# The first stage of a decoder layer with x in token layout instead of feature layout, and without GpSimd

## The chip, the cores and the metric

The kernel runs on one NeuronCore of a Trainium2 chip, as one launch. The metric is the device time of that launch in microseconds (us). A launch has five engines with queues of their own: TensorE (PE in the profile; its weight loads are PEld), VectorE (DVE), ScalarE (ACT), GpSimd (POOL) and SyncE (SP, which here only issues transfers). Work on different engines is ordered by semaphores alone.

## The reference

One layer (DEPTH is 1) of a decoder trunk on 512 tokens of 1024 features in float32: an adaptive norm, a token mixer (block-sparse attention beside a gated delta rule), a second adaptive norm, a mixture of 32 experts, and a final norm. What matters here is how it begins:

```python
c_act = jax.nn.silu(c)
mod = (c_act @ w_mod[l] + b_mod[l])[:, None, :]
sh1, sc1, g1, sh2, sc2, g2 = jnp.split(mod, N_MOD, axis=-1)
h = rms_norm(x, norm1_w[l]) * (1.0 + sc1) + sh1
# token_mixer(h, ...):
proj = h @ w_in
```

where `rms_norm(x, w)` is `x * rsqrt(mean(x * x) + EPS) * w`, the mean taken over the 1024 features of a token. `w_mod` is 1024 x 6144, and the first 2048 of its columns give `sh1` and `sc1`; `w_in` has 6408 columns.

## The kernel before

The kernel is written in a framework that sets the semaphores itself. It also orders each engine's queue: an instruction may move ahead of others that were written earlier, if its inputs are ready by the framework's own reckoning. `tc.issue_after(i)` holds the instructions of a block behind instruction `i` on the engine of `i`; it sets an order in the queue and is no wait for data.

The program is `mixer` (L805), then the mixture of experts. `mixer` begins with `front` (L223), the stage that is changed. The front makes h for all 512 tokens and multiplies it with the first 768 columns of `w_in`: 512 for the values of the attention, 2 x 128 for the first key and query of the delta rule. What follows is a sequence of units of 128 columns of `w_in` (`unit_in`, L369 and on): 24 matmuls each, into PSUM tiles named `pj`.

Products with `w_in` are made at more than the precision of one pass: each factor is split into a high part of a shorter type (fp32r) and a low part, the rest, and three matmuls are summed: high x high, high x low, low x high (`mm3`, L136). h is kept so as `hhi` and `hlo`, and each piece of the weight as `gh` and `gl`.

The front works in feature layout: the features lie on the partitions, in 8 pieces of 128, and the tokens along the rows.

- x is loaded transposed (`xT`, 128 x 8 x 512) in four transfers of 512 KB, in turn on ScalarE's and SyncE's queue (L248). A row of c, the constants and small columns follow, and then on SyncE's queue, for each piece k, 1 MB of `w_mod` (four buffers, `mr`) and 384 KB of `w_in` (three buffers, `gr`; `w_first` in the profile), L252. After these come the loads of the units (L363).
- c is spread over the partitions by TensorE (L260), and two Silus give `cact` (L273).
- The squares of x's pieces are made on ScalarE (L266) and VectorE (L264), summed in part on VectorE (L268, L270) and over the partitions by TensorE, with a column of ones (L280). `F1` = 12 products before that, `F2` = 5 and `F3` = 8 after it have no result that is used: they keep TensorE's clock up (`warm`, L211).
- The norms come out as 4 columns of 128 tokens, `rs` (L285 to L287). TensorE turns them into rows on all partitions (L292), and ScalarE copies these to `rB` (L293).
- Then a loop over the 8 pieces (L301). For each: ScalarE makes `gh` (L306) and GpSimd `gl` (L307); VectorE makes two products with accumulation over 1024 elements, which are the entries of `mod` for this piece (`mod_tile`, L217 to L220), and two small instructions that give scale and shift (`A1`, L312; `sh1`, L314); GpSimd multiplies the piece of x with `rB` (L317; for piece 0 VectorE does, L321); ScalarE makes h twice, once as `hhi` (L326) and once in full (L327), and VectorE the difference, `hlo` (L328). TensorE does 18 matmuls of 128x128 by 128x512: 12 into `accv` (L332 to L334), 6 into `accf` through `mm3` (L138 to L140).

At the end ScalarE copies `accv` out (L341), and small loads for what follows are issued from ScalarE's queue (L339).

`rsqrt` (L146) is a root on ScalarE and four small instructions on VectorE; `split` (L142) is the pair of ScalarE and VectorE instructions that makes a weight's parts in the later units (L143, L144).

Of the kernel before, what the change touches and what calls it, by code (L numbers as in the profile page):

```python
# [9 lines left out]
F32 = mybir.dt.float32  # L10
# [4 lines left out]
AF = mybir.ActivationFunctionType  # L15
OP = mybir.AluOpType
# [4 lines left out]
D = 1024  # L21
S = 512
EPS = 1e-6
# [12 lines left out]
NU = 18  # L36
SPL = 4
XL = 1
F1, F2, F3 = 12, 5, 8
BA, BB = 0, 1  # L40


# [51 lines left out]
class Prog:  # L94
# [128 lines left out]
    def front(self):  # L223
        tc, nc, I, V = self.tc, self.nc, self.ins, self.view
        v = nc.vector
        mm = nc.tensor.matmul
        pp = self.pf
        hR = self.arena(self.open("H", "right"), "hR", 32, F32R)
        self.hhi, self.hlo = V(hR, 0, [8, 512]), V(hR, 16, [8, 512])
        mp = self.open("MISC", "right")  # L230
        mi = self.arena(mp, "misc", 12)
        self.cm = mp.tile([128, C_W - C_W1], F32, name="cm")
        self.negm = self.cm[:, C_NEG - C_W1:]
        self.va = V(mi, 0, [4, 512])
# [3 lines left out]
        xT = V(sF, 0, [8, 512])  # L238
        rB, nt = V(sF, 16, [512]), V(sF, 18, [512])
        mr = [V(sF, 20 + 8 * i, [2, 1024]) for i in range(4)]  # L240
        gr = [V(sF, 52 + 3 * i, [768]) for i in range(3)]
        sq = [V(sF, 61 + 2 * i, [512]) for i in range(8)]
        one = V(sF, 77, [128])
        crow = V(sF, 78, [1024])[:1]
        v.memset(one, 1.0)
        nc.scalar.activation(nt[:1, 1:2], one[:1, 0:1], AF.Silu)
        nc.sync.dma_start(crow, I["c"])
        for k in range(0, 8, 2):  # L248
            (nc.scalar, nc.sync)[k // 2 % 2].dma_start(xT[:, k:k + 2], I["xT"][:, k:k + 2])
        self.first_loads()  # L250

        def loads(k):  # L252
            if k >= 8:
                return
            nc.sync.dma_start(mr[k % 4], I["w_mod1"][k])
            nc.sync.dma_start(gr[k % 3], I["w_first"][k])
        pc = []
        for b in range(2):
            pc.append(pp.tile([128, 512], F32, name="tr", bufs=2))
            mm(pc[b], one[:1], crow[:, 512 * b:512 * b + 512], start=True, stop=True)  # L260

        for k in range(8):
            if k in (1, 3, 5):
                v.tensor_mul(sq[k], xT[:, k], xT[:, k])  # L264
            else:
                nc.scalar.activation(sq[k], xT[:, k], AF.Square)  # L266
            if k % 2:
                m0 = v.tensor_add(sq[k - 1], sq[k - 1], sq[k])  # L268
            if k in (3, 5):
                m0 = v.tensor_add(sq[0], sq[0], sq[k - 1])  # L270
            if k == 3:
                for b in range(2):
                    nc.scalar.activation(self.cact[:, 512 * b:512 * b + 512], pc[b], AF.Silu)  # L273
        nc.scalar.activation(nt[:1, 0:1], one[:1, 0:1], AF.Sqrt)
        p = pp.tile([128, 512], F32, name="tr", bufs=2)
        w = self.warm(p, one, F1)
        with tc.issue_after(w.ins):
            for t in range(4):
                for k in (0, 6):
                    w = mm(p[:, t:t + 1], sq[k][:, t * 128:(t + 1) * 128], one[:, 0:1], start=k == 0, stop=k == 6)  # L280
        loads(0)
        with tc.issue_after(m0.ins):
            self.mod_tile(0, mr[0][:, 0])
        ss, rs = self.pool.tile([128, 4], F32, name="ss1"), self.pool.tile([128, 4], F32, name="rs1")
        v.tensor_scalar(ss, p[:, 0:4], 1.0 / D, EPS, op0=OP.mult, op1=OP.add)  # L285
        mS = nc.scalar.activation(rs, ss, AF.Sqrt)
        m0 = self.rsqrt(rs, ss, "1", self.pool.tile([128, 4], F32, name="nt1"), root=False)  # L287
        p = pp.tile([128, 4, 128], F32, name="tr", bufs=2)
        with tc.issue_after(w.ins):
            w = self.warm(p[:, 0], one, F2)  # L290
            for t in range(4):
                w = nc.tensor.transpose(p[:, t], rs[:, t:t + 1].to_broadcast([128, 128]), self.ident)  # L292
        mB = nc.scalar.activation(rB, p.rearrange("p a b -> p (a b)"), AF.Copy)  # L293
        accv = [pp.tile([128, 512], F32, name=f"accv{t}") for t in range(4)]
        accf = [pp.tile([128, 512], F32, name=f"accf{t}") for t in range(2)]
        with tc.issue_after(w.ins):
            w = self.warm(accv[0], one, F3)
        ml = None
        with tc.issue_after(m0.ins):
            v.tensor_scalar(self.b1, self.bmod[:, 8:16], 1.0, None, op0=OP.add)  # L300
        for k in range(8):  # L301
# [3 lines left out]
            with tc.issue_after(mB.ins if k else mS.ins):  # L305
                nc.scalar.activation(gh, g, AF.Copy)  # L306
            ml, mg = nc.gpsimd.tensor_tensor(gl, g, gh.bitcast(F32), op=OP.subtract), ml  # L307
            with tc.issue_after(m0.ins):
# [3 lines left out]
            v.tensor_scalar(self.A1[:, k:k + 1], self.mod[:, 8 + k:9 + k], self.b1[:, k:k + 1],  # L312
                            self.n1[:, k:k + 1], op0=OP.add, op1=OP.mult)
            v.tensor_add(self.sh1[:, k:k + 1], self.mod[:, k:k + 1], self.bmod[:, k:k + 1])  # L314
            if k:
                with tc.issue_after(mg.ins):
                    nc.gpsimd.tensor_tensor(xT[:, k], xT[:, k], rB, op=OP.mult)  # L317
            else:
                for a in range(4):
                    c = slice(128 * a, 128 * a + 128)  # L320
                    m0 = v.tensor_mul(xT[:, k, c], xT[:, k, c], p[:, a])  # L321
            h = sq[k]
            ab = dict(scale=self.A1[:, k:k + 1], bias=self.sh1[:, k:k + 1])
            for a in range(1 if k else 4):
                c = slice(0, 512) if k else slice(128 * a, 128 * a + 128)
                nc.scalar.activation(self.hhi[:, k, c], xT[:, k, c], AF.Identity, **ab)  # L326
            m1 = nc.scalar.activation(h, xT[:, k], AF.Identity, **ab)  # L327
            v.tensor_sub(self.hlo[:, k], h, self.hhi[:, k].bitcast(F32))  # L328
            for t in range(4):
                ts = slice(t * 128, t * 128 + 128)  # L330
                with tc.issue_after(w.ins):
                    mm(accv[t], self.hhi[:, k, ts], gh[:, 0:512], start=(k == 0), stop=False)  # L332
                mm(accv[t], self.hhi[:, k, ts], gl[:, 0:512], start=False, stop=False)
                mm(accv[t], self.hlo[:, k, ts], gh[:, 0:512], start=False, stop=(k == 7))  # L334
            for j in range(2):
                cs = slice(512 + 128 * j, 640 + 128 * j)
                self.mm3(accf[j], gh[:, cs], gl[:, cs], self.hhi[:, k], self.hlo[:, k], k == 0, k == 7)
# [1549 lines left out]
```

## Time and profile before

| what | value |
|---|---|
| time, median of 3 runs | 743.18 us (742.13 to 745.19) |
| the profiled execution: its time, its span | 742.16 us, 740.0 us |
| mean granted clock of TensorE, as a share | 0.989 |
| TensorE busy | 707.5 us (96%) |
| VectorE busy | 507.3 us (69%) |
| ScalarE busy | 283.2 us (38%) |
| GpSimd busy | 88.2 us (12%) |
| moved by DMA | 183.11 MB, mean 247 GB/s |
| first and last instruction of the front's loop on TensorE | 18.65 us, 66 us |

A row of the groups gives line, engine, operation, tiles, shape and count, then the busy time in us, the mean of one in ns, and the idle time of the engine just before, with the engine that ended it. A row of the timeline gives start and duration in us, then the same names, and in brackets the idle time before and what ended it. `x4` at the end of a row of the timeline means four instructions merged. A matmul of full f32 shows as two records, one of fp32r as one. In the windows each engine's busy time has the number of its instructions behind it, and the last three columns are granted clock, share of the 16 DMA engines and GB/s. The tile names are those of the memory areas: `sF` holds x, the pieces of `w_mod` and `w_first` and h in full, `sR` the parts of the weight, `hR` those of h, `misc` `cact`.

### The profile page before, as it was taken

Reading aid. Unit: us, or ns where it says so; the run is one execution under the profiler, and the core shown is the slowest. Engines: PE = TensorE matmul, PEld = TensorE weight load, DVE = VectorE, ACT = ScalarE, POOL = GpSimd, SP = SyncE. Lnnn points to the kernel's source line nnn. Section 1 sums busy time; section 2 is a strip of 40 time slices with the busy share of each in tenths; the row PEclk is TensorE's granted clock in tenths of the full one; section 3 lists DMA queues with packets and bytes.
Section 4 is the critical chain, followed back from the end, with each engine's and each line's share of the span. In section 5 each row is a group of like instructions: output and inputs, shape, how many; then the busy total and the mean of one; then the engine's idle time right before and its main releaser. Section 6 shows DMA issues by size and latency. Waiting matters only on the chain. (4 is left out here: it accounts for less than half of the span.)

```text
span 740.0 us, 11015 instructions
## 1 busy us (share of the span) xinstructions
PE 707.5 (96%) x3949; PEld 482.3 (65%) x3949; DVE 507.3 (69%) x1241; ACT 283.2 (38%) x546; POOL 88.2 (12%) x70
## 2 busy tenths in 40 slices
PE   7889999999999989999999999999999999999995
PEld 6657768778877778876768886796444444454431
DVE  5998668987746675668885754256687766677653
ACT  4335445853333312447673233333322222232252
POOL 1863000240222300000000000101010000000000
PEclk9899999999999999999999999999999999999998
DMA  9733222118877661171128897456999999999993
GB/s 357 304 140 116 85 86 86 58 36 286 269 232 279 221 229 58 58 271 42 58 81 292 313 404 315 159 190 240 371 408 409 405 407 411 413 413 406 422 415 153
DMA packets 47515, 183.11 MB, mean 247 GB/s; under 512 B 11802, under 2 KB 13370, under 8 KB 34018
## 3 DMA queue, kind: packets, MB, share of 16 engines
q1 hardware_dynamic: 40690, 169.91, 60.9%
q10 hardware_dynamic: 4896, 8.25, 3.1%
q0 software_dynamic: 1872, 4.23, 1.5%
q8 instruction: 32, 0.52, 0.3%
q14 instruction: 25, 0.20, 0.1%
HBM read 175.63 MB, written 9.33 MB: 250 GB/s over the span
## 5 line engine op out<-in xcount | busy, mean ns | idle before, releaser
L138 PE MATMUL pj<-hR,uR 128*128 128x512 f32 x304 | 122.6, 403 | 1.5 <-DVE qk L736 1.5
L140 PE MATMUL pj<-hR,uS 128*128 128x512 f32 x304 | 122.6, 403 | 0.0
L139 PE MATMUL pj<-hR,uR 128*128 128x512 f32 x304 | 122.4, 403 | 0.0
L143 ACT ACTIVATE uR<-uF 128x1024 fp32r<-128x1024 f32 x48 | 50.8, 1059 | 92.7 <-PE pj L139 81.5
L144 DVE TENSOR_TENSOR uS<-uF,uR 128x1024 fp32r<-128x1024 f32 x48 | 59.7, 1244 | 25.2 <-ACT uR L143 24.8
L1824 DVE TENSOR_TENSOR accF<-accF,cb 128x512 f32<-128x512 f32 x96 | 60.3, 682 | 21.1 <-PE cb L1823 19.9
L1750 PE MATMUL gu<-ra,uS 128*64 128x512 f32 (+1 forms) x344 | 70.2, 597 | 0.0
L138 PEld LDWEIGHTS pj<-hR,uR 128*128 128x128 f32 x304 | 57.3, 189 | 13.6 <-issue 2.7
L140 PEld LDWEIGHTS pj<-hR,uS 128*128 128x128 f32 x304 | 57.3, 189 | 12.6 <-DVE uS L144 1.3
L139 PEld LDWEIGHTS pj<-hR,uR 128*128 128x128 f32 x304 | 57.3, 189 | 11.5 <-issue 0.3
L219 DVE SCALAR_TENSOR_TENSOR sgF<-sgF,misc 128x1024 f32<-128x1024 f32 x32 | 40.1, 1258 | 19.4 <-DMA sgF<-w_mod 19.1
L1750 PEld LDWEIGHTS gu<-ra,uS 128*64 128x64 f32 (+1 forms) x344 | 19.1, 123 | 34.7 <-issue 33.9
L1822 PE MATMUL cb<-uR,oht 128*128 128x512 f32 x96 | 41.1, 428 | 0.0
L1823 PE MATMUL cb<-uR,oht 128*128 128x512 f32 x96 | 37.8, 394 | 0.0
L1807 PE MATMUL cb<-ra,uS 128*32 128x512 f32 (+1 forms) x160 | 36.5, 597 | 0.6 <-ACT uS L1789 0.5
L1812 ACT ACTIVATE uR<-p2F 128x512 fp32r<-128x512 f32 x24 | 15.1, 630 | 56.3 <-DVE p2F L1809 56.3
L1775 ACT ACTIVATE uS<-gu 128x256 f32<-128x256 f32 x13 | 5.0, 384 | 82.3 <-PE gu L1750 82.3
L1636 POOL DMA_INDIRECT uF<-xd,idx x12 | 12.5, 1039 | 180.2 <-PE tr L1671 121.6
L1780 DVE SCALAR_TENSOR_TENSOR uS<-uS,meta,gu 128x256 f32<-128x256 f32 x13 | 6.2, 481 | 34.1 <-ACT uS L1775 34.0
L1750 PE MATMUL gu<-rb,uS 128*32 128x512 f32 (+1 forms) x184 | 29.1, 595 | 0.0
L219 DVE SCALAR_TENSOR_TENSOR sF<-sF,misc 128x1024 f32<-128x1024 f32 x16 | 27.7, 1740 | 0.0
L138 PE MATMUL pj<-mR,uR 128*128 128x512 f32 (+1 forms) x72 | 27.3, 379 | 0.0
(440 smaller groups left out, 1474.8 us busy)
## 6 DMA issues: line engine op xcount, KB each, us to landing
ra<-w_e SPq DMA_DIRECT2D x55, 1024.0 KB, 8.6
rb<-w_e SPq DMA_DIRECT2D x25, 1024.0 KB, 9.4
uF<-w_in SPq DMA_DIRECT2D x38, 512.0 KB, 3.4
sgF<-w_mod SPq DMA_DIRECT2D x32, 512.0 KB, 4.2
rc<-w_e SPq DMA_DIRECT2D x15, 1024.0 KB, 9.1
sF<-w_mod SPq DMA_DIRECT2D x8, 1024.0 KB, 9.0
gd<-sgF ACTq DMA_DIRECT2D x16, 256.0 KB, 2.9
gF<-gd SPq DMA_DIRECT2D x8, 512.0 KB, 3.6
```

The source lines that it names most:

```text
L138: mm(ps, whi, xhi, start=first, stop=False)
L139: mm(ps, whi, xlo, start=False, stop=False)
L140: mm(ps, wlo, xhi, start=False, stop=last)
L143: self.nc.scalar.activation(hi, raw, AF.Copy)
L144: self.nc.vector.tensor_sub(lo, raw, hi.bitcast(F32))
L219: self.nc.vector.scalar_tensor_tensor(raw, raw, 1.0, self.cact, op0=OP.mult, op1=OP.mult, accum_out=self.mod[:, ot:ot + 1])
L1750: nc.tensor.matmul(gu[r], xe[:, k, r], w[:, k % 4], start=k == 0, stop=k == 7)
L1807: nc.tensor.matmul(dn[h][r], aT[:, f, r], w[:, f, c], start=f == 0, stop=f == 1)
L1812: i1 = nc.scalar.activation(self.yhi[:, c], self.yf[:, c], AF.Copy)
L1822: nc.tensor.matmul(pc, self.oht[:, ts], self.yhi[:, c], start=True, stop=False)
L1823: nc.tensor.matmul(pc, self.oht[:, ts], self.ylo[:, c], start=False, stop=True)
L1824: nc.vector.tensor_add(self.acc[:, t, c], self.acc[:, t, c], pc)
```

## The change

x is loaded in token layout (`xr`, 128 tokens x 4 x 1024 features), again in four transfers of 512 KB on the same two queues.

- The sum of squares of a token is then a sum along its row: VectorE makes it for three of the four pieces of 128 tokens, ScalarE for the third, each in one instruction with accumulation. The root's table is loaded behind ScalarE's. The two Silus of c now stand ahead of ScalarE's square.
- The norms stay in token layout: neither ones nor rows of norms are needed. x is scaled by its tokens' norms in two ways. For feature pieces 0 and 1 TensorE multiplies x with a diagonal matrix of the norms (`dg`, four ScalarE instructions), which turns and scales at once, in f32. For pieces 2 to 7 ScalarE scales x in place, in steps 1 to 3 of the loop, two pieces at a time (four instructions 128x256), and TensorE transposes.
- A turned piece lies in PSUM (`tr`, two buffers), and ScalarE makes `hhi` and the full h from there. Piece k + 1 is turned in step k, behind the first six matmuls.
- `gl` is made by VectorE. In its queue it stands behind `A1` and `sh1` of its own step, and the next step's products stand behind it. GpSimd has no work in the front.
- The 18 matmuls of a step are in another order: six high x high, then the four transposes, six high x low, six low x high; all of TensorE's queue in the loop is fixed by hand.
- The warming products are `F1` = 8 ahead of the first turning and `F2` = 10 behind it; the third group is gone. `hf` holds full h in four buffers instead of eight. `xT` is still an input, for use after the mixer.

The diff, cut to its core:

```diff
-F1, F2, F3 = 12, 5, 8
+F1, F2 = 8, 10
...
-        for k in range(0, 8, 2):
-            (nc.scalar, nc.sync)[k // 2 % 2].dma_start(xT[:, k:k + 2], I["xT"][:, k:k + 2])
+        for t in range(4):
+            (nc.scalar, nc.sync)[t % 2].dma_start(xr[:, t], I["xr"][:, t])
...
+        for b in range(2):
+            w = nc.scalar.activation(self.cact[:, 512 * b:512 * b + 512], pc[b], AF.Silu)
+
+        ss, rs = self.pool.tile([128, 4], F32, name="ss1"), self.pool.tile([128, 4], F32, name="rs1")
+        for t in range(4):
+            if t == 2:
+                with tc.issue_after(w.ins):
+                    mS = nc.scalar.activation(jk[0], xr[:, t], AF.Square, accum_out=ss[:, t:t + 1])
             else:
-                nc.scalar.activation(sq[k], xT[:, k], AF.Square)
...
+                v.scalar_tensor_tensor(jk[1], xr[:, t], 1.0, xr[:, t], op0=OP.mult, op1=OP.mult,
+                                       accum_out=ss[:, t:t + 1])
+        with tc.issue_after(mS.ins):
+            nc.scalar.activation(nt[:1, 0:1], one[:1, 0:1], AF.Sqrt)
         loads(0)
...
+        v.tensor_scalar(ss, ss, 1.0 / D, EPS, op0=OP.mult, op1=OP.add)
+        m0 = self.rsqrt(rs, ss, "1", self.pool.tile([128, 4], F32, name="nt1"))
+        for t in range(4):
+            mS = nc.scalar.activation(dg[:, t], self.ident, AF.Copy, scale=rs[:, t:t + 1])
...
+        def turned(k):
+
+            xp[k] = p = pp.tile([128, 512], F32, name="tr", bufs=2)
+            for t in range(4):
+                a, o = xr[:, t, 128 * k:128 * k + 128], p[:, 128 * t:128 * t + 128]
+                if k < 2:
+                    i = mm(o, a, dg[:, t], start=True, stop=True)
+                else:
+                    i = nc.tensor.transpose(o, a, self.ident)
+            return i
+        w = self.warm(accv[0], one, F1)
         with tc.issue_after(w.ins):
-            w = self.warm(accv[0], one, F3)
-        ml = None
+            turned(0)
+            w = turned(1)
+        with tc.issue_after(w.ins):
+            w = self.warm(accv[0], one, F2)
...
-            ml, mg = nc.gpsimd.tensor_tensor(gl, g, gh.bitcast(F32), op=OP.subtract), ml
-            with tc.issue_after(m0.ins):
+            with tc.issue_after(last.ins):
                 for j in range(2):
-                    if k + j:
-                        self.mod_tile(8 * j + k, m[:, j])
...
+                    self.mod_tile(8 * j + k, m[:, j])
...
+            h = hf[k % 4]
+            with tc.issue_after(i.ins), tc.issue_after(j.ins):
+                last = v.tensor_sub(gl, g, gh.bitcast(F32))
+            nc.scalar.activation(self.hhi[:, k], xp[k], AF.Identity, **ab)
+            mS = m1 = nc.scalar.activation(h, xp[k], AF.Identity, **ab)
+            if 0 < k < 4:
+
+                c = slice(256 * k, 256 * k + 256)
+                with tc.issue_after(m1.ins):
+                    for t in range(4):
+                        mS = nc.scalar.activation(xr[:, t, c], xr[:, t, c], AF.Copy, scale=rs[:, t:t + 1])
             v.tensor_sub(self.hlo[:, k], h, self.hhi[:, k].bitcast(F32))
...
+            for a, b, st, sp in ((hi, gh, k == 0, False), (hi, gl, False, False), (lo, gh, False, k == 7)):
+                for t in range(4):
+                    with tc.issue_after(w.ins):
+                        w = mm(accv[t], a[:, k, ts[t]], b[:, 0:512], start=st, stop=sp)
+                for j in range(2):
+                    with tc.issue_after(w.ins):
+                        w = mm(accf[j], b[:, cs[j]], a[:, k], start=st, stop=sp)
+                if b is gh and a is hi and 0 < k < 7:
+                    with tc.issue_after(w.ins):
+                        w = turned(k + 1)
...
+    a["xr"] = f["x"][0].reshape(4, 128, 1024).transpose(1, 0, 2)
```

More of the change, by code (lines that the diff above doesn't have):

```diff
@@ L237, in front @@
         sF, sR = self.arena(st, "sF", 84), self.arena(st, "sR", 18, F32R)
-        xT = V(sF, 0, [8, 512])
-        rB, nt = V(sF, 16, [512]), V(sF, 18, [512])
+        xr = V(sF, 0, [4, 1024])
+        dg, nt = V(sF, 16, [4, 128]), V(sF, 18, [512])
         mr = [V(sF, 20 + 8 * i, [2, 1024]) for i in range(4)]
         gr = [V(sF, 52 + 3 * i, [768]) for i in range(3)]
-        sq = [V(sF, 61 + 2 * i, [512]) for i in range(8)]
+        hf = [V(sF, 61 + 2 * i, [512]) for i in range(4)]
+        jk = [V(sF, 69 + 4 * i, [1024]) for i in range(2)]
         one = V(sF, 77, [128])
@@ L260, in front @@
             mm(pc[b], one[:1], crow[:, 512 * b:512 * b + 512], start=True, stop=True)
-        for k in range(8):
-            if k in (1, 3, 5):
-                v.tensor_mul(sq[k], xT[:, k], xT[:, k])
-            else:
[L266 to L280, printed above, removed]
-        loads(0)
-        with tc.issue_after(m0.ins):
-            self.mod_tile(0, mr[0][:, 0])
-        ss, rs = self.pool.tile([128, 4], F32, name="ss1"), self.pool.tile([128, 4], F32, name="rs1")
@@ L285, in front @@
[L285 to L292, printed above, removed]
@@ L293, in front @@
-        mB = nc.scalar.activation(rB, p.rearrange("p a b -> p (a b)"), AF.Copy)
+        for b in range(2):
[5 more added lines that the diff above has]
+                    mS = nc.scalar.activation(jk[0], xr[:, t], AF.Square, accum_out=ss[:, t:t + 1])
+            else:
+                v.scalar_tensor_tensor(jk[1], xr[:, t], 1.0, xr[:, t], op0=OP.mult, op1=OP.mult,
+                                       accum_out=ss[:, t:t + 1])
@@ L298, in front @@
-        ml = None
+            turned(0)
+            w = turned(1)
+        with tc.issue_after(w.ins):
+            w = self.warm(accv[0], one, F2)
         with tc.issue_after(m0.ins):
             v.tensor_scalar(self.b1, self.bmod[:, 8:16], 1.0, None, op0=OP.add)
+        last = m0
         for k in range(8):
@@ L304, in front @@
             gh, gl = V(sR, 6 * (k % 3), [768]), V(sR, 3 + 6 * (k % 3), [768])
-            with tc.issue_after(mB.ins if k else mS.ins):
+            with tc.issue_after(mS.ins):
                 nc.scalar.activation(gh, g, AF.Copy)
-            ml, mg = nc.gpsimd.tensor_tensor(gl, g, gh.bitcast(F32), op=OP.subtract), ml
-            with tc.issue_after(m0.ins):
+            with tc.issue_after(last.ins):
                 for j in range(2):
-                    if k + j:
-                        self.mod_tile(8 * j + k, m[:, j])
@@ L312, in front @@
[L312 to L321, printed above, removed]
@@ L322, in front @@
-            h = sq[k]
-            ab = dict(scale=self.A1[:, k:k + 1], bias=self.sh1[:, k:k + 1])
[L324 to L334, printed above, removed]
@@ L335, in front @@
-            for j in range(2):
-                cs = slice(512 + 128 * j, 640 + 128 * j)
-                self.mm3(accf[j], gh[:, cs], gl[:, cs], self.hhi[:, k], self.hlo[:, k], k == 0, k == 7)
+                    self.mod_tile(8 * j + k, m[:, j])
+            j = v.tensor_scalar(self.A1[:, k:k + 1], self.mod[:, 8 + k:9 + k], self.b1[:, k:k + 1],
+                                self.n1[:, k:k + 1], op0=OP.add, op1=OP.mult)
+            i = v.tensor_add(self.sh1[:, k:k + 1], self.mod[:, k:k + 1], self.bmod[:, k:k + 1])
@@ new lines, in front @@
+            v.tensor_sub(self.hlo[:, k], h, self.hhi[:, k].bitcast(F32))
+            ts = [slice(t * 128, t * 128 + 128) for t in range(4)]
+            cs = [slice(512 + 128 * j, 640 + 128 * j) for j in range(2)]
+            hi, lo = self.hhi, self.hlo
+            for a, b, st, sp in ((hi, gh, k == 0, False), (hi, gl, False, False), (lo, gh, False, k == 7)):
[8 more added lines that the diff above has]
+                        w = turned(k + 1)
```

1 line of the change is left out of this document (added).

## The prediction

> **What bounds the kernel now.** I read the page first, then its windows cut at the borders of the front, then the groups of instructions inside the front with their shapes kept apart, and last the timeline.
>
> ```profile
> span 740.0 us, 11015 instructions
> ```
>
> The profiled execution took 742.16 us, 2.2 us around a span of 740.0; the median of the three runs is 743.18, so 1.0 us is added at the end to a sum made on this execution.
>
> ```profile
> 18.65:65.99 47.34, 39.46 (x145) 29.70 (x145) 43.76 (x67) 20.65 (x31) 29.85 (x15) 0.89 0.53 197
> 65.99:480.00 414.01, 405.18 (x2072) 317.23 (x2071) 285.20 (x669) 180.27 (x338) 42.29 (x38) 1.00 0.51 177
> ...
> 520.00:720.00 200.00, 199.46 (x1284) 89.68 (x1281) 135.20 (x320) 56.35 (x125) 10.26 (x10) 1.00 1.00 409
> ```
>
> The columns are the stretch, its length, busy time of PE, PEld, DVE, ACT and POOL, the granted clock, the DMA share and GB/s. From 18.65 (first matmul of the front's loop) to 65.99 (first matmul behind it) VectorE is busy 43.8 of 47.3 us, while TensorE idles 7.9 us and has a clock of 0.89. Everywhere else TensorE fills the time: 405 of 414 us, then 199 of 200. So the front is the one long stretch that TensorE does not pace, and the question is what paces it.
>
> ```profile
> L219 DVE SCALAR_TENSOR_TENSOR sF<-sF,misc 128x1024 f32<-128x1024 f32 x16 | 27.7, 1740 | 0.0
> L307 POOL TENSOR_TENSOR sR<-sF,sR 128x768 fp32r<-128x768 f32 x8 | 19.1, 2392 | 26.7 <-DVE rs L156 15.8 <-issue 8.3 <-ACT sR L306 2.5
> L314 DVE TENSOR_TENSOR sh<-mod,c_cols 128x1 f32<-128x1 f32 x8 | 9.0, 1120 | 0.0
> ...
> L306 ACT ACTIVATE sR<-sF 128x768 fp32r<-128x768 f32 x8 | 6.6, 830 | 0.0
> L327 ACT ACTIVATE sF<-sF,sh,A 128x512 f32<-128x512 f32 x8 | 6.4, 801 | 0.0
> ```
>
> ```profile
> 25.70 1.21 DVE L219 SCALAR_TENSOR_TENSOR sF<-sF,misc 128x1024 f32<-128x1024 f32 x1
> 26.85 1.22 DVE L219 SCALAR_TENSOR_TENSOR sF<-sF,misc 128x1024 f32<-128x1024 f32 x1
> 28.00 0.68 DVE L328 TENSOR_TENSOR hR<-sF,hR 128x512 fp32r<-128x512 f32 x1
> 28.22 2.14 POOL L307 TENSOR_TENSOR sR<-sF,sR 128x768 fp32r<-128x768 f32 x1 [2.45 <-ACT sR L306]
> 28.60 0.26 DVE L312 TENSOR_SCALAR A<-mod,b,c_cols 128x1 f32<-128x1 f32 x1
> 28.78 1.59 DVE L314 TENSOR_TENSOR sh<-mod,c_cols 128x1 f32<-128x1 f32 x1
> ...
> 33.14 2.86 DVE L219 SCALAR_TENSOR_TENSOR sF<-sF,misc 128x1024 f32<-128x1024 f32 x1
> ...
> 60.41 0.15 DVE L314 TENSOR_TENSOR sh<-mod,c_cols 128x1 f32<-128x1 f32 x1
> 60.52 0.27 DVE L312 TENSOR_SCALAR A<-mod,b,c_cols 128x1 f32<-128x1 f32 x1
> 60.71 1.21 DVE L144 TENSOR_TENSOR uS<-uF,uR 128x1024 fp32r<-128x1024 f32 x1
> ```
>
> The two products at 25.70 and 26.85, with GpSimd idle, take 1.15 us from start to start; the one at 33.14, beside GpSimd's subtraction, takes 2.86. A 128x1 addition takes 0.15 at 60.41 and 1.59 at 28.78, where GpSimd had started 0.56 before. VectorE's instructions are stretched whenever GpSimd runs: 16 x (1.74 - 1.22) = 8.3 us on the products and 8 x (1.12 - 0.15) = 7.8 on the small additions, 16 of its 44 busy us. The additions give the shift that ScalarE needs for h, so each stretched one delays h and with it TensorE.
>
> ```profile
> 24.69 2.08 PE L334 MATMUL accv<-sR,hR 128*128 128x512 f32 x4 [3.21 <-DVE hR L328]
> ...
> 33.20 0.39 PE L140 MATMUL accf<-hR,sR 128*128 128x512 f32 x1
> ...
> 35.92 0.39 PE L334 MATMUL accv<-sR,hR 128*128 128x512 f32 x1
> ...
> 50.54 0.50 PE L332 MATMUL accv<-sR,hR 128*128 128x512 f32 x1 [2.00 <-ACT hR L326]
> ...
> 51.26 0.63 PE L332 MATMUL accv<-sR,hR 128*128 128x512 f32 x1
> ...
> 51.69 0.63 PE L333 MATMUL accv<-sR,hR 128*128 128x512 f32 x1
> ```
>
> ```profile
> 25.00:30.00 5.00, 5.00 (x13) 3.89 (x13) 5.00 (x8) 2.25 (x3) 2.55 (x2) 0.50 0.79 297
> ...
> 50.00:55.00 5.00, 4.46 (x13) 3.50 (x14) 4.49 (x8) 1.93 (x3) 2.94 (x2) 0.66 0.00 0
> ```
>
> At full clock 12 matmuls start between 33.20 and 35.92: 0.227 us each. The loop's 144 then cost 32.6 us. The other 14.7 of 47.3 are 7.9 of idling and 6.8 that come with it: after the waits of 3.21 and 2.00 us the clock falls to half, and a matmul takes 0.43 (51.26 to 51.69).
>
> **The change, part by part.**
>
> *GpSimd leaves.* Its 8 subtractions go to VectorE, its 7 products with the norm disappear: x is now scaled by its own row, and ScalarE and TensorE do that. VectorE's step, unstretched, is two products 2.30, A1 and shift 0.30, h's low part 0.60 (28.00 to 28.60) and a new subtraction of 128x768. That shape is not in the trace on VectorE; it lies between 0.68 (512 wide) and 1.21 (1024 wide), midway 0.95. Sum 4.15 a step, 33.2 for eight.
>
> *ScalarE's step.* The split of the weight 0.83, two makings of h at 0.80 each. h now comes from PSUM; the nearest rows give 0.80 (the same form from SBUF) and 0.60 below (a plain 128x512 copy from PSUM), so 2.0 to 2.4. In steps 1 to 3 four scalings 128x256 come on top:
>
> ```profile
> L768 ACT ACTIVATE aF<-aF,sm 128x256 f32<-128x256 f32 x8 | 4.0, 504 | 0.4 <-DVE sm L767 0.4
> ```
>
> 2.0 us at most, hence 4.4 in three of the steps. What is queued behind them is the next weight split; VectorE's subtraction waits for that, but I expect slack there (below).
>
> *TensorE's step.* The 18 matmuls stay, in another order: 4.08 us. Steps 1 to 6 add four transposes each, turning the next piece.
>
> ```profile
> 156.12 1.14 ACT L617 ACTIVATE dF<-ax,nk 128x128 f32<-128x128 f32 x4 [3.42 <-PE ax L615]
> ...
> 156.62 1.47 PE L615 MATMUL ax<-ct,dF 128*128 128x128 f32 x12
> ```
>
> Twelve such take 1.47, so four 0.49. A full step is 4.57 us, above VectorE's 4.15 and ScalarE's 4.4: **TensorE becomes the pace of the loop**. Eight steps: 32.6 + 6 x 0.49 = 35.6 us. Waits that the new order brings are covered: the transposes of step 1 follow six matmuls (1.4 us) and wait for ScalarE's scalings, 0.8 + 2.0 us behind h's high part of that step; that high part is ready long before TensorE gets there, because TensorE starts late (next paragraph). If the cover were gone it would cost 1.4 us, once. GpSimd's subtraction as a wait of the weight queue goes too:
>
> ```profile
> SPq L256 <- POOL sR L307: 26.3, 5, 7.0
> ...
> SPq L975 <- PE gu L1750: 63.8, 22, 7.0
> ```
>
> The loads of w_first stood 26.3 us in SP's queue behind it, and the w_in loads behind them; both come earlier. The count and sizes of x's loads, and their two queues, are as before.
>
> *The start.*
>
> ```profile
> 2.29 3.75 PE L260 MATMUL tr<-sF 1*128 1x512 f32 x4 [2.29 <-DMA sF<-c]
> ...
> 7.01 1.06 ACT L273 ACTIVATE misc<-tr 128x512 f32<-128x512 f32 x2
> ...
> 7.64 5.49 PE L214 MATMUL tr<-sF 128*128 128x128 f32 x24 [1.61 <-ACT misc L273]
> 7.96 1.67 ACT L266 ACTIVATE sF<-sF 128x512 f32<-128x512 f32 x3
> ...
> 9.65 1.28 ACT L274 ACT_TABLE_LOAD   x1
> ...
> 15.02 0.16 DVE L285 TENSOR_SCALAR ss<-tr 128x4 f32<-128x4 f32 x1 [2.39 <-PE tr L280]
> ...
> 16.06 0.16 DVE L156 SCALAR_TENSOR_TENSOR rs<-nt,rs 128x4 f32<-128x4 f32 x1
> ...
> 16.77 1.95 PE L214 MATMUL accv<-sF 128*128 128x128 f32 x16
> ```
>
> The row sums need no TensorE any more. All of x is in by about 8.5 (the second of the three squares from 7.96 reads the last piece). VectorE's last square ends near 9.7. ScalarE's stands behind the two Silus, which end at 8.07: about 1.2 us for 1024 elements, then the table load of 1.28, at 10.6. From the scaled sum to the norm the chain takes 16.22 - 15.02 = 1.2, of which 0.2 lies before the root: norm at 11.8 instead of 16.2. Four diagonals follow at 1.14/4 each, the first ready at 12.1. Then TensorE has 18 f32 products of 128x128 in a fixed order ahead of the loop (turning pieces 0 and 1, and ten that only warm the clock). One costs 1.95/8 = 0.244 at full clock and 5.49/12 = 0.457 in the cold start. Bounds: all warm 4.4 us, loop from 16.5 (h is ready by 11.8 + 2 x 1.15 + 0.5 + 0.8 = 15.4). But TensorE has idled over 2 us by then, and the windows show half clock for 3.4 us (a clock of 0.66 over 5 us) to over 5 us after such waits: 3.4 us of cold, then full, gives 6.0; 5.3 gives 6.9; loop from 18.1 to 19.0. Worse still: the eight warming products F1 depend only on a memset and may run ahead of the products with c, which start at 2.29; that can delay those, the Silus and the norm by up to 8 x 0.457 - 1.3 = 2.4, loop from 21.4. I take 19.0, beside the 18.65 of before: what the early norm gains, the warming eats.
> The Trainium skill ("TensorE: Matmul & The Clock Gate", Part 1) says that the clock is halved after at least one idle window of about 3.4 us and released after about 3.4 us of sustained work. The trace halves it after only 2.00 us of idling, and shows the 3.4 us once and a longer stretch once; by the page's release time the loop would start at 18.1 and the result be 0.9 us lower.
>
> *Sum.* 19.0 + 35.6 = 54.6 against 65.99: 11.4 us. Behind it, VectorE's and ScalarE's splits of the first w_in units fall due at the same distance before the end of the loop, and they have slack. The stages after are TensorE's own (405 of 414 us). Between 520 and 720 the DMA share is 1.00 at 409 GB/s, but those loads are issued when TensorE's work frees their buffers (the SP row with gu above), so they move with it. 742.16 - 11.4 = 730.8, and 1.0 for the median: **731.8 us**.
>
> **Rivals.**
> 1. *VectorE's queue stays serial.* If the next step's products are queued behind h's low part and the subtraction, a step is h 0.8, low part 0.6, subtraction 0.95, products 2.3, A1 and shift 0.3, h's high part 0.8: 5.75. TensorE would then end near 15.4 + 7 x 5.75 + 4.1 = 59.8: 6.2 us gained, 737.0. Against it: in the trace the next products run ahead of h's low part. Chance 0.10.
> 2. *The gain is lost later*, because a later stretch is tied to transfers (DMA 1.00 over 200 us): half, 737.5. For it speaks that share, against it the issue waits. Chance 0.07.
> 3. *The change does not do what it says*: VectorE's stretching comes from the DMA's writes, not from GpSimd. Then VectorE keeps its 5.5 us a step (43.8/8) and gets 0.95 more: 11.8 + 8 x 6.45 + 2 = 65.4, no change, 743. Against it: the rows at 25.70 and 26.85 are short, with the DMA share of 0.79 in that window. Chance 0.05.
> 4. *Slower: the half clock.* If the weight split also gets into the serial chain (it is queued behind h and behind the scalings), a step is 5.75 + 0.83 = 6.6, TensorE idles 2.0 us in every step, and 2.00 was enough for the clock to fall. It then stays low: 18 x 0.43 + 0.5 = 8.2 us a step, 19.0 + 66 = 85, 19 us slower, 762. It decides from 6.6 us a step on. Chance 0.06. By the same section of the Trainium skill it would take 3.4 us of idling, so a step of 8 us, and this rival would be all but excluded; the measured 2.00 keeps it in.
>
> **How the numbers follow.** The forecast has 0.72: its own range runs from a loop start at 16.5 (729.3) to one at 21.4 (734.2), widened by the runs' spread to 728.3 to 735.5. The first two rivals, 737.0 and 737.5, are faster as well. The range must leave out no more than two in ten; up to 738.0 it holds all but rivals 3 and 4 and some of the tails. 0.5%, which is about what a measurement of this kernel can tell from no change, is 3.7 us. Faster 0.88, same 0.06, slower 0.06.
>
> **What would show it.** Right: no GpSimd work between 1 and 54 us; the products with w_mod at 1.2 us, the shift additions at 0.15; TensorE busy without a gap from about 19 to 55 at a clock of 1.00; the first matmul on w_in near 55 instead of 66, and the same 674 us behind it. Wrong: products still at 1.7; waits of TensorE for h over 1 us in each step; half clock inside the loop; a transpose that waits for ScalarE's scalings; or a tail that grew.

## The result and the profile after

The changed kernel took 731.6 us (median of 4 runs, 728.54 to 733.87) beside 742.98 us for the kernel before (4 runs): 11.4 us less, a ratio of 0.984 with a 95% interval of 0.982 to 0.987. Two later comparisons of the same two kernels gave 0.983 [0.980, 0.986] and 0.981 [0.977, 0.985].

The first two lines of the page after are the span and the busy time of each engine:

```profile
span 732.1 us, 11015 instructions
...
PE 702.7 (96%) x3955; PEld 483.2 (66%) x3955; DVE 495.8 (68%) x1242; ACT 286.0 (39%) x555; POOL 54.9 (7%) x55
```

The profiled execution took 733.87 us; it was the slowest of the four, at a mean granted clock of 0.988 where the other three had 0.994 to 0.997, and why it was is a question of its own below. GpSimd has 33 us less to do than before. VectorE has 11.5 us less although it took over GpSimd's eight subtractions. Now the windows, cut as in the prediction: the loop of the front, the units behind it, a stretch of the experts (length, PE, PEld, DVE, ACT, POOL, clock, DMA share, GB/s):

```profile
17.08:52.76 35.68, 35.68 (x172) 29.48 (x170) 31.55 (x71) 22.16 (x36) 0.00 (x0) 1.00 0.76 296
52.76:467.00 414.24, 403.58 (x2055) 317.26 (x2054) 285.98 (x668) 179.82 (x339) 41.20 (x38) 0.99 0.51 176
507.00:707.00 200.00, 197.25 (x1266) 89.73 (x1266) 135.76 (x319) 54.99 (x125) 10.25 (x10) 1.00 0.99 403
```

In the loop TensorE is busy for all of the 35.68 us, at a clock of 1.00. Before it was busy for 39.5 of 47.3 us at 0.89. So TensorE paces the loop now, and VectorE has 4 us to spare. In the two other stretches TensorE is still busy nearly all the time; that it is a little less so than before (403.6 of 414 us at a clock of 0.99, and 197.3 of 200) belongs to the question of what this execution lost behind the front. The groups of the first 53 us, shapes kept apart, show what became of VectorE's instructions:

```profile
L219 DVE SCALAR_TENSOR_TENSOR sF<-sF,misc 128x1024 f32<-128x1024 f32 x16 | 19.2, 1219 | 0.0
...
L318 DVE TENSOR_TENSOR sR<-sF,sR 128x768 fp32r<-128x768 f32 x8 | 7.6, 953 | 0.4 <-ACT sR L308 0.4
...
L319 ACT ACTIVATE hR<-tr,sh,A 128x512 fp32r<-128x512 f32 x8 | 6.2, 780 | 10.9 <-PE tr L292 7.8 <-DVE A L312 3.1
...
L314 DVE TENSOR_TENSOR sh<-mod,c_cols 128x1 f32<-128x1 f32 x8 | 1.2, 152 | 0.0
```

The sixteen products fell from 1740 to 1219 ns, the eight shift additions from 1120 to 152 ns, and the subtraction of 128x768 that came to VectorE takes 953 ns. The same in VectorE's timeline, one step of the loop:

```profile
15.18 1.22 DVE L219 SCALAR_TENSOR_TENSOR sF<-sF,misc 128x1024 f32<-128x1024 f32 x1
...
16.32 0.69 DVE L327 TENSOR_TENSOR hR<-sF,hR 128x512 fp32r<-128x512 f32 x1
16.93 1.22 DVE L219 SCALAR_TENSOR_TENSOR sF<-sF,misc 128x1024 f32<-128x1024 f32 x1
...
18.07 0.15 DVE L314 TENSOR_TENSOR sh<-mod,c_cols 128x1 f32<-128x1 f32 x1
...
18.38 0.95 DVE L318 TENSOR_TENSOR sR<-sF,sR 128x768 fp32r<-128x768 f32 x1
19.25 1.22 DVE L219 SCALAR_TENSOR_TENSOR sF<-sF,misc 128x1024 f32<-128x1024 f32 x1
```

A step is 4.07 us (15.18 to 19.25), and the first product of the next step is issued ahead of the low part of h: the queue is not serial. Last, TensorE's timeline:

```profile
1.06 3.36 PE L214 MATMUL accv<-sF 128*128 128x128 f32 x14 [1.06 <-DVE sF L246]
4.35 1.98 PE L261 MATMUL tr<-sF 1*128 1x512 f32 x4
...
11.71 3.38 PE L290 MATMUL tr<-sF 128*128 128x128 f32 x16 [4.96 <-ACT sF L279]
14.93 2.40 PE L214 MATMUL accv<-sF 128*128 128x128 f32 x20
17.08 1.17 PE L334 MATMUL accv<-sR,hR 128*128 128x512 f32 x4
...
22.63 0.60 PE L292 MATMUL tr<-ct,sF 128*128 128x128 f32 x4
...
52.76 0.39 PE L138 MATMUL pj<-hR,uR 128*128 128x512 f32 x1
```

The last row is the first matmul on `w_in` behind the front: 52.76 instead of 65.99, a gain of 13.2 us at that point. Only 7.9 us of it are left in the span of this execution (740.0 to 732.1). So 5.3 us were given back on the way, and that had to be explained.

### The profile page after: what moved, and what is told of

The parts are those of the page before. It is cut to its first block, busy times and chain, and to the rows that moved or that the text cites. A ratio compares the mean times of both kernels' runs of the same rounds, so it can differ in the third digit from the quotient of the medians.

```text
span 732.1 us, 11015 instructions
## 1 busy us (share of the span) xinstructions
PE 702.7 (96%) x3955; PEld 483.2 (66%) x3955; DVE 495.8 (68%) x1242; ACT 286.0 (39%) x555; POOL 54.9 (7%) x55
## 5 line engine op out<-in xcount | busy, mean ns | idle before, releaser
L139 PEld LDWEIGHTS pj<-hR,uR 128*128 128x128 f32 x304 | 57.6, 189 | 11.6 <-issue 0.3
L219 DVE SCALAR_TENSOR_TENSOR sgF<-sgF,misc 128x1024 f32<-128x1024 f32 x32 | 41.9, 1316 | 18.3 <-DMA sgF<-w_mod 18.2
L1815 ACT ACTIVATE uR<-p2F 128x512 fp32r<-128x512 f32 x24 | 15.1, 630 | 56.2 <-DVE p2F L1812 56.2
L409 DVE SCALAR_TENSOR_TENSOR dF<-dF,c_cols 128x512 f32<-128x512 f32 x36 | 26.5, 748 | 0.9
L140 PE MATMUL pj<-mR,uS 128*128 128x512 f32 (+1 forms) x72 | 27.0, 375 | 0.0
```

The lines of the kernel that those rows point to most:

```text
L139: mm(ps, whi, xlo, start=False, stop=False)
L140: mm(ps, wlo, xhi, start=False, stop=last)
L219: self.nc.vector.scalar_tensor_tensor(raw, raw, 1.0, self.cact, op0=OP.mult, op1=OP.mult, accum_out=self.mod[:, ot:ot + 1])
L409: nc.vector.scalar_tensor_tensor(a, r[:, k:k + 512], w[:, k:k + 1], a, op0=OP.mult, op1=OP.add)
```

## The experiments

Three questions were open: what stretched VectorE, how much each half of the change brings, and where the 5.3 us went. A fourth came with the start of the loop. The ratio is to the runs of the kernel before in the same comparison; the three last columns, in us, come from one profiled execution each; "tail" is the span less the front's end, that is, all that lies behind the first matmul on `w_in`.

| kernel | median, us (runs) | ratio to before | loop starts | front ends | tail |
|---|---|---|---|---|---|
| before | 742.98 (4) | 1 | 18.65 | 65.99 | 674.0 |
| after | 731.60 (4) | 0.984 [0.982, 0.987] | 17.08 | 52.76 | 679.3 |
| after_again | 730.89 (6) | 0.983 [0.980, 0.986] | 18.44 | 54.11 | 674.4 |
| pool_beside | 748.28 (5) | 1.007 [1.004, 1.009] | 22.24 | 72.50 | 673.4 |
| feature_dve | 732.98 (4) | 0.987 [0.983, 0.990] | 18.71 | 57.62 | 673.5 |
| short_warm | 728.82 (4) | 0.980 [0.977, 0.983] | 15.90 | 52.56 | 676.7 |
| sub_on_pool | 733.92 (4) | 0.988 [0.986, 0.990] | 17.18 | 56.10 | 674.3 |
| pool_one_input | 745.63 (10) | 1.004 [1.002, 1.005] | 20.95 | 68.66 | 674.6 |
| warm_bridge | 729.60 (5) | 0.983 [0.981, 0.986] | 15.59 | 51.78 | 674.3 |
| no_warm | 729.35 (4) | 0.982 [0.980, 0.984] | 15.47 | 51.51 | 673.3 |
| after_third | 730.29 (6) | 0.981 [0.977, 0.985] | 18.07 | 53.74 | 675.0 |
| no_warm_again | 728.28 (6) | 0.980 [0.976, 0.984] | 15.85 | 51.80 | 673.4 |

**The changed kernel once more** (after_again, no edit): does the give-back belong to the change or to that one execution?

> The changed kernel once more, with five rounds and a second profile. In the first profile the front ended 13.2 us earlier than before, but the span was only 7.9 us shorter: 5.3 us were given back, 4.5 of them in the stage that inverts the triangular blocks, where TensorE waited 2.40 and 2.06 us and the clock fell to half twice. Theory: that is a matter of each execution's transfers and clock windows, not of the change; this profile gives back under 3 us there, the time is 728 to 733, and the front ends at 52.8 again within 0.3. Rival: the earlier front makes the inversion collide with the loads of w_mod in every execution; then this profile gives back 4 to 5 us there again, at the same two waits.

The tail was 674.4 us, 0.4 more than before's; it was 675.0 in a third profile. So the give-back does not come with every execution of the change, and the medians keep the whole gain: they lie 13.2 and 13.6 us below the kernel before in the two later comparisons, where the fronts end 11.9 and 12.3 us earlier. What the first profile had lost can be read: two waits of TensorE for VectorE in the inversion of the triangular blocks of the delta rule. Behind both stands a load: shortly before, a product with `w_mod` in VectorE's queue had waited 1.20 and 3.02 us for its transfer. First after's rows, those of VectorE ahead of those of TensorE, and then the windows of 6 us around the waits:

```profile
236.93 1.23 DVE L219 SCALAR_TENSOR_TENSOR sgF<-sgF,misc 128x1024 f32<-128x1024 f32 x1 [1.20 <-DMA sgF<-w_mod]
...
254.35 1.23 DVE L219 SCALAR_TENSOR_TENSOR sgF<-sgF,misc 128x1024 f32<-128x1024 f32 x1 [3.02 <-DMA sgF<-w_mod]
```

```profile
238.81 0.66 PE L608 MATMUL ax<-ct,dF 128*128 128x128 f32 x4 [2.40 <-DVE dF L605]
...
256.50 0.49 PE L650 MATMUL ax<-dF 128*128 128x128 f32 x2 [2.06 <-DVE dF L647]
```

```profile
238.00:244.00 6.00, 5.18 (x28) 4.80 (x29) 3.41 (x8) 1.20 (x2) 1.38 (x1) 0.72 0.64 214
256.00:262.00 6.00, 5.50 (x26) 4.89 (x27) 3.71 (x9) 0.00 (x0) 0.00 (x0) 0.72 0.56 182
```

The clock was 0.72 in both windows, which costs up to 0.28 x 6 = 1.7 us in each. The repeat has the first of these waits too, almost as long, and its clock stays full:

```profile
239.96 0.66 PE L608 MATMUL ax<-ct,dF 128*128 128x128 f32 x4 [2.27 <-DVE dF L605]
```

```profile
239.00:245.00 6.00, 5.04 (x36) 4.43 (x37) 4.35 (x8) 1.79 (x3) 2.68 (x2) 1.00 0.63 215
```

Two falls of the clock are 3.4 us; one wait for a weight of the experts near 697 us, 1.4 us in the first profile and 0.2 in the repeat, is 1.2; that makes 4.6 us, and TensorE's waits in the inversion are 7.2 us in sum in the first profile and 6.2 in the repeat, one more. The tails differ by 4.9, so the parts are right to about a microsecond. That the earlier front has no part in such waits is not shown: waits of over 2 us stand in this stage in four profiles with the changed front (after, after_again, short_warm, sub_on_pool) and not in the one profile of before, whose longest is 1.03. Whether a wait of 2 us costs the clock is no matter of its length alone. The Trainium skill ("TensorE: Matmul & The Clock Gate", Part 1) says that the window in which activity is counted runs freely and so meets the same kernel in another phase each time. That fits 2.27 us at a clock of 1.00 beside 2.40 us at 0.72; its figure of 3.4 us of idling does not fit this trace, which has idle times of 2.40 and 2.06 there.

The expected front's end was missed, by 1.3 us. The rows of TensorE in the repeat show why:

```profile
4.34 3.78 PE L261 MATMUL tr<-sF 1*128 1x512 f32 x4
...
12.69 3.76 PE L290 MATMUL tr<-sF 128*128 128x128 f32 x16 [3.84 <-ACT sF L279]
...
18.44 1.17 PE L334 MATMUL accv<-sR,hR 128*128 128x512 f32 x4
```

The products with c took 3.78 us instead of 1.98: here they ran at half clock, and Silu, norm and turning came 1 us later. The start of the loop is not fixed to better than about 1.4 us.

**GpSimd's work put back, on other data** (pool_beside): is it GpSimd that stretches VectorE's instructions, or the DMA's writes (rival 3)? Nothing of the computation changes; nobody reads the results of the added instructions.

```diff
+        for n in range(16):
+            c = slice(0, (768, 512)[n % 2])
+            nc.gpsimd.tensor_tensor(jk[1][:, c], jk[1][:, c], jk[0][:, c], op=OP.subtract)
         last = m0
```

> The changed kernel, and beside its loop 16 GpSimd subtractions of the two sizes that GpSimd had before (8 of 128x768, 8 of 128x512), on data that nothing else uses, so that no instruction waits for GpSimd. Theory (GpSimd's running alone stretches VectorE, and that paced the front): the products with w_mod go from 1.22 to about 1.7 us each while GpSimd works, VectorE's loop gets 10 to 18 us longer, TensorE waits again, the front ends at 58 to 66 instead of 52.8 and the time is 736 to 744. Rival (what cost was waiting for GpSimd's results, or the late norm, or the order of the matmuls; the stretching is the DMA's): the front ends at 53 to 54 and the time stays within 2 us of the changed kernel's.

The front ended at 72.50, and the kernel is slower than before. Its groups in the front and its window of the loop:

```profile
L219 DVE SCALAR_TENSOR_TENSOR sF<-sF,misc 128x1024 f32<-128x1024 f32 x16 | 25.7, 1624 | 0.0
...
L304 POOL TENSOR_TENSOR sF<-sF 128x768 f32<-128x768 f32 x8 | 18.1, 2257 | 10.1 <-DVE sF L271 9.6
...
L317 DVE TENSOR_TENSOR sh<-mod,c_cols 128x1 f32<-128x1 f32 x8 | 5.5, 682 | 0.0
```

```profile
22.24:72.50 50.26, 40.83 (x171) 32.13 (x170) 46.52 (x75) 22.52 (x37) 20.13 (x10) 0.90 0.50 181
```

One of the small instructions that make the norm, ahead of the loop:

```profile
10.04 1.80 DVE L276 TENSOR_SCALAR ss<-ss 128x4 f32<-128x4 f32 x1
```

Nobody waits for the added work, and yet the products are back at 1.62 us and the additions at 0.68. The loop takes 50.3 us instead of 35.7, with 9.4 us of waits of TensorE for h and a clock of 0.90, much as before the change. All of these waits lie before 43.1, where the added work ends; behind that TensorE is busy without a gap. The DMA share in the loop is lower than after's (0.50 against 0.76). So the stretching is GpSimd's, and rival 3 falls. The size was underestimated, though VectorE's busy time in the loop grew by 15.0 us, within the 10 to 18 expected. The front ends 19.7 us later than after's, and the expectation left out two parts of that: the loop starts 5.2 us later (22.24 against 17.08), since the added work meets the norm's small instructions as well (1.80 us at 10.04 where the changed kernel has 0.16; the norm is ready at 15.1 against 11.2), and a clock of 0.90 over 50.3 us is about 5.0 us. The waits are the other 9.4.

**The old layout without GpSimd** (feature_dve): the kernel before, in which VectorE makes the subtraction and the product of x with the norms.

```diff
-            ml, mg = nc.gpsimd.tensor_tensor(gl, g, gh.bitcast(F32), op=OP.subtract), ml
+                    v.tensor_mul(xT[:, k], xT[:, k], rB)
...
-                    nc.gpsimd.tensor_tensor(xT[:, k], xT[:, k], rB, op=OP.mult)
+                last = v.tensor_sub(gl, g, gh.bitcast(F32))
```

> The kernel before in its feature layout, with one part of the change alone: GpSimd's subtractions and its products with the norms go to VectorE. Theory: VectorE's step is then 4.15 + 0.61 = 4.76 us, without stretching, from the norm at 16.2 on: eight steps, h 0.8 and the last 18 matmuls 4.1 end the front at 58 to 59, so 7 to 8 us of the 13.2 come from freeing VectorE alone and the time is about 735. The layout gives the rest: the earlier norm, and the product with the norm off VectorE. Rival (the token layout, with its early norm and the new matmul order, is what gains): the front ends at 63 to 67 and the time is 740 to 744.

The window of its loop, and two rows of VectorE's timeline one step apart:

```profile
18.71:57.62 38.91, 36.27 (x145) 26.09 (x145) 37.18 (x75) 21.39 (x31) 0.00 (x0) 1.00 0.66 240
```

```profile
27.98 0.95 DVE L322 TENSOR_TENSOR sR<-sF,sR 128x768 fp32r<-128x768 f32 x1
...
32.64 0.95 DVE L322 TENSOR_TENSOR sR<-sF,sR 128x768 fp32r<-128x768 f32 x1
```

VectorE is busy 37.2 of 38.9 us: it still paces the loop, at 4.66 us a step, but unstretched and with no half clock. The front ended 8.4 us earlier than before (57.62), a little better than expected. In time the kernel is at 732.98, 2.1 us behind the changed one of the same comparison, with intervals that overlap. So in the old layout, too, taking GpSimd's work away brings most of the gain.

**The new layout with GpSimd's subtraction** (sub_on_pool): the other half alone.

```diff
-            with tc.issue_after(i.ins), tc.issue_after(j.ins):
-                last = v.tensor_sub(gl, g, gh.bitcast(F32))
+            last = i
+            nc.gpsimd.tensor_tensor(gl, g, gh.bitcast(F32), op=OP.subtract)
```

> The changed kernel with one part undone: the 8 subtractions that make the low part of the weight are on GpSimd again, 2.0 to 2.4 us each; the products with the norm stay away from it. Theory (a VectorE instruction beside a GpSimd one takes up to as long as the GpSimd one): VectorE loses 8 x 0.87 = 7.0 us of its own work and gains about 0.5 us of stretching for each of 16 to 19 us of GpSimd, 8 to 9.5; its loop stays near TensorE's 35.7, so the front ends at 53 to 58 and the time is 730 to 736. Rival (any two-input work of GpSimd brings the old pace back): the front ends above 60, the time is above 738.

The front ended at 56.10, within what was expected. One collision in the timelines of VectorE and GpSimd:

```profile
28.31 1.21 DVE L219 SCALAR_TENSOR_TENSOR sF<-sF,misc 128x1024 f32<-128x1024 f32 x1
...
29.45 1.79 DVE L314 TENSOR_TENSOR sh<-mod,c_cols 128x1 f32<-128x1 f32 x1
```

```profile
28.95 2.28 POOL L318 TENSOR_TENSOR sR<-sF,sR 128x768 fp32r<-128x768 f32 x1 [1.11 <-ACT sR L308]
```

The product was running when GpSimd began at 28.95, and kept its 1.21 us. The 128x1 addition behind it started in the middle of GpSimd's instruction and ended at 31.24; GpSimd ended at 31.23. It waited that instruction out. In the groups the additions are stretched as before the change (mean 1128 ns), the products much less (1316 instead of 1740). Either half alone ends the front 8 to 10 us earlier, both together 12 to 13: the halves overlap. Either takes GpSimd's product with the norms away, and with both TensorE's 35.7 us set the loop, so that what VectorE has to spare counts for nothing.

**GpSimd work with one input** (pool_one_input): is it two inputs on GpSimd's side that matter?

```diff
+        for n in range(24):
+            nc.gpsimd.tensor_copy(jk[1], jk[0])
         last = m0
```

> The changed kernel, and beside its loop 24 GpSimd copies of 128x1024 on data that nothing else uses. Each reads one tensor instead of two. Theory (what GpSimd and VectorE get in each other's way with is the reading of two tensors): the products with w_mod stay at 1.22 us, the front ends at 52.5 to 54.5, the time stays within 2 us of the changed kernel's. Rival (any GpSimd work on SBUF stretches VectorE): the products take 1.5 us and more, the front ends above 58 and the time is above 735, as with the 16 subtractions, which gave 72.5 and 748.

The groups in the front:

```profile
L303 POOL COPY sF<-sF 128x1024 f32<-128x1024 f32 x24 | 36.8, 1535 | 11.2 <-DVE sF L271 9.7
...
L219 DVE SCALAR_TENSOR_TENSOR sF<-sF,misc 128x1024 f32<-128x1024 f32 x16 | 26.7, 1686 | 0.0
...
L316 DVE TENSOR_TENSOR sh<-mod,c_cols 128x1 f32<-128x1 f32 x8 | 4.5, 562 | 0.0
...
L314 DVE TENSOR_SCALAR A<-mod,b,c_cols 128x1 f32<-128x1 f32 x8 | 2.1, 264 | 0.0
```

My theory fell: plain copies on GpSimd stretch VectorE's products to 1.69 us and cost the whole gain (745.63). So two inputs on GpSimd's side are not needed, and what remains is VectorE's side. Its two-tensor instructions wait, while `A1`, which reads one tensor and two scalars by pointer, stays at 0.26 us beside any GpSimd work in these fronts. The number of tensors is not the whole rule, though. The one-tensor instruction at 10.04 in pool_beside took 1.80 us instead of 0.16, and behind the front, in the changed kernel itself, a one-tensor instruction of 128x512 (L407, at 55.26) that meets a GpSimd memset takes 2.03 us, where the median of its line is 0.48. What tells such instructions from `A1` was not tested. The Trainium skill ("GPSIMD Engine Reference", section 8) says that the two engines share their interfaces to SBUF, the memory of the tiles, and that VectorE's instructions contend which have two SBUF inputs or run in a 2-port perf mode. The two-tensor rows agree with it; the mode of an instruction no trace here shows. The size of the effect is what these runs add.

**The warming products.** Three kernels change only their numbers. short_warm cuts the group between turning and loop:

```diff
-F1, F2 = 8, 10
+F1, F2 = 8, 1
```

> The changed kernel with one warming product instead of ten behind the first turning (F2 = 1). In the first profile h's first piece was ready at 15.3, but TensorE did the warming until 17.0. Theory: the loop starts at 15.3, the clock is already full by then (it rose at 14.5), the front ends 1.7 us earlier, at 51.1, and the time is 1 to 2 us lower. Rival: the ten products are what brings the clock up; without them the loop's first 3.4 us or more run at half clock, and the front ends at 52.8 or later.

The loop's first rows:

```profile
12.04 3.78 PE L290 MATMUL tr<-sF 128*128 128x128 f32 x16 [5.29 <-ACT sF L279]
...
15.90 2.05 PE L334 MATMUL accv<-sR,hR 128*128 128x512 f32 x4
```

The loop started at 15.90, but its first four matmuls took 2.05 us instead of 1.17: the clock was still at half. So the end was 52.56 and not the 51.1 expected. The long tail of this profile, 676.7, is like that of the first: TensorE waited 2.88 us for VectorE ahead of 240.11, and the clock was 0.58 over 240 to 244. warm_bridge makes the wait for x itself warm instead:

```diff
-F1, F2 = 8, 10
+F1, F2 = 24, 5
```

> The changed kernel with 24 and 5 warming products instead of 8 and 10: 17 of the 24 fill TensorE's time between c's products and the first turning. With one product behind the turning the loop had started at 15.9 but ran its first 2 us at half clock. Theory: the clock is full from about 8 us on, the turning takes 2.0 instead of 3.4 us, the loop starts when h is there, at 15.3 to 16.5, at full clock, the front ends at 51.0 to 52.2 and the time is 727.5 to 729.5. Rival: the 17 products run at half clock, 7.8 us, and hold the turning up; the loop starts at 18 or later and nothing is gained against the changed kernel.

```profile
6.15 5.69 PE L214 MATMUL accv<-sF 128*128 128x128 f32 x34
12.01 2.05 PE L290 MATMUL tr<-sF 128*128 128x128 f32 x16 [0.17 <-ACT sF L279]
...
15.59 1.21 PE L334 MATMUL accv<-sR,hR 128*128 128x512 f32 x4 [0.41 <-ACT hR L319]
```

That held: the turning takes 2.05 us at full clock instead of 3.4 to 3.8, and TensorE then waits 0.41 us for h, so this is the earliest start that h allows here; the front ended at 51.78. The time, 729.60, is just above the 727.5 to 729.5 expected. no_warm has almost no warming at all:

```diff
-F1, F2 = 8, 10
+F1, F2 = 1, 1
```

> The changed kernel with one warming product in each place instead of 8 and 10. Theory (warming only decides where the half clock falls): c's products run at half clock, 3.7 us, from 2.3; the turning runs at half clock, the loop starts at 15.5 to 16.5 and its first 3 to 6 us run at half clock, which costs 1.5 to 3 us; the front ends at 52.5 to 55 and the time is 729 to 733. Rival (the warming is what the front needs): the clock stays low for long, TensorE falls behind, the front ends above 57.

```profile
2.27 3.78 PE L261 MATMUL tr<-sF 1*128 1x512 f32 x4 [0.42 <-DMA sF<-c]
11.61 3.78 PE L290 MATMUL tr<-sF 128*128 128x128 f32 x16 [5.56 <-ACT sF L279]
15.19 0.64 PE L214 MATMUL accv<-sF 128*128 128x128 f32 x2
15.47 1.51 PE L334 MATMUL accv<-sR,hR 128*128 128x512 f32 x4
```

It was better than expected: 51.51. The products with c start at 2.27 instead of 4.35, since nothing stands ahead of them; they and the turning run mostly at half clock, but that holds nothing up: ScalarE makes h's high part from 14.45 on, and what it waits for last is VectorE's `A1`, not the turned piece. At 15.47 h is there and the loop starts at once. The cold costs 0.34 us on the first four matmuls. The changed kernel and this one were then compared once more, side by side:

> The changed kernel beside the one without warming products, on the same chip. Both theories: front end at 52.5 to 54.2, time 729.5 to 731.5.

> The changed kernel with one warming product in each place, beside the changed kernel on the same chip. Its front ended at 51.5, 1.2 to 2.6 us earlier than in the two profiles of the changed kernel. Theory (ten warming products stand between the turned piece and the loop, and hold up what they were to speed up): the front ends at 51.3 to 52.5 again, the time is 1 to 2.5 us below the changed kernel's of this call. Rival (the clock's windows decide, and the first profile was a lucky one): the front ends at 53 or later, the times are within 0.7 us of each other.

The medians were 730.29 and 728.28 us, and the fronts ended at 53.74 and 51.80, all as expected, with ratios to before whose intervals overlap. Over all profiles the front ends at 51.5 and 51.8 without warming, and at 52.8, 54.1 and 53.7 with it; over all runs the medians are 728.9 (10 runs) and 730.6 (16 runs). That a version with almost no warming beats the changed kernel by 1.7 to 2 us is shown by the front's end, and only weakly by the time.

## Why the prediction was right

The forecast of 731.8 us stands against 731.6, with the two later medians at 730.9 and 730.3. That it is met to 0.2 us is luck: the runs of the changed kernel spread from 727.7 to 733.9, and the gain, 11.4 us in the forecast, was 11.4, 13.2 and 13.6 us in the three comparisons. The mechanism held. Its steps, one by one:

- *GpSimd stretches VectorE, and that paces the front.* Shown: removing the work ends it, adding unrelated work brings it back, and in sub_on_pool one addition ends 0.01 us behind the GpSimd instruction that it met. The trace of before says the same: the addition at 28.78 ends at 30.37, GpSimd's subtraction at 30.36, and each of the seven products of 1.62 us and more ends 1.08 or 1.09 us behind the GpSimd instruction that it met. So it is not, as the prediction put it, that VectorE is stretched whenever GpSimd runs: a two-tensor instruction waits once, until GpSimd's current one is done (the one at 30.30, begun just before GpSimd's next, takes 1.21). It works the other way round too, which the prediction overlooked. All eight GpSimd subtractions of before met a two-tensor instruction of VectorE and ended 1.66 to 1.71 us behind it, so their mean of 2.39 us holds waiting of their own. One of them, begun while a product was running that ended at 53.05:

```profile
51.83 1.22 DVE L219 SCALAR_TENSOR_TENSOR sF<-sF,misc 128x1024 f32<-128x1024 f32 x1
52.06 2.67 POOL L307 TENSOR_TENSOR sR<-sF,sR 128x768 fp32r<-128x768 f32 x1 [2.68 <-issue]
```

- *VectorE's step of 4.15 us, with 0.95 for a shape that the trace of before lacked.* Measured 4.07 and 0.95. The value midway between the two neighbouring widths was exact.
- *ScalarE's h from PSUM at 0.60 to 0.80, the scalings at most 2.0.* Measured 0.78 and 0.77, and 1.70 for four. Piece 2 is scaled at 21.60 and TensorE turns it at 22.63 without a wait: the cover that the prediction named is there, 1.0 us thick. In warm_bridge, where TensorE comes earlier, the same four transposes take 1.02 instead of 0.60 us.
- *TensorE becomes the pace, 35.6 us.* Measured 35.68, and 35.67 in both repeats. Within this the four transposes cost 0.36 us, not 0.49 (22.63 to the next matmul at 22.99), and the matmuls 0.233 each, (35.68 - 6 x 0.36) / 144, not 0.227; the two cancel.
- *The loop starts at 19.0.* This term was mis-sized, by 0.6 to 1.9 us: 17.08, 18.44 and 18.07. The norm was ready at 11.2 in the first profile and at 12.2 in the repeats (11.8 was reckoned; the prediction's own figures give 11.6, since 0.2 of its 1.2 us lies ahead of the root and does not follow the table load). The cold clock costs the 18 products 5.4 to 5.8 us, where 6.0 to 6.9 were reckoned. The warming products did run ahead of the products with c, as feared, and held them up by 2.1 us (4.35 against 2.27 in no_warm). In the first profile this came back at once, since they then ran at full clock (1.98 instead of 3.78); in the repeats it cost 1 us. The bounds of 16.5 to 21.4 held.
- *The same 674 us behind it.* True of the repeats (674.4 and 675.0) and of most other kernels (673.3 to 674.6), not of short_warm's profile, 676.7, nor of the first one, 679.3. In the first profile the error of 1.9 us in the start and the give-back of 5.3 us had opposite signs.

Of the rivals, the serial queue was not seen (next product at 15.18 ahead of the low part at 16.32). Of the loss in a later stretch tied to transfers the first profile has a part (VectorE's waits for `w_mod`, and 1.4 us for a weight of the experts), but it is no rule: the tail of no_warm, whose front ends 14.5 us earlier than before's, is 673.3. The DMA as the cause was refuted by pool_beside. The half clock inside the loop did not come; it is what pool_beside shows when the step grows (clock 0.90), and there the kernel is indeed slower than before.

What stays open: which one-tensor instructions of VectorE wait for GpSimd, whether the earlier front makes the long waits of the inversion likelier, and why a wait of some 2 us costs the clock in one execution and not in another.

## What to carry to other kernels

An engine that is off the bound can still set it: when VectorE's two-tensor instructions are long where GpSimd runs and short where it does not, look for instructions that end together with GpSimd's, charge VectorE with what it waits there (16 us by the rows in the prediction, where GpSimd was busy for 32.5 in the front), and consider that work moved from GpSimd to VectorE can make VectorE's load smaller, here by 11.5 us. Price warming products like any other work in a queue, by what they hold up: here they cost the front's end more than the cold clock that they avoid. Before a gain that "was given back" is explained, take a second profile and compare the tails.

## What was not expected of the hardware

- A VectorE instruction with two tensors that starts while GpSimd works waits for the end of GpSimd's current instruction, whatever its own size (128x1: 1.79 us instead of 0.15; 128x1024: 2.86 instead of 1.22); one already running is not touched (1.21). GpSimd's copies with a single input do it as well, and GpSimd's subtractions wait for VectorE in the same way (2.67 us at 52.06 in the kernel before, 1.68 of them behind the product's end).
- Waits of about 2.3 us on TensorE were followed by half clock in one execution (2.40, then 0.72 over 6 us) and not in another (2.27, then 1.00).
